# Gate and up of two feed-forwards: weights moving, three of eight feature pairs by seven block products, inner features in two halves

## Chip, cores and metric

One core of a Trainium2 chip. The metric is the device time of one execution in microseconds (us); lower is better. The core's engines are TensorE (PE in the profile, its weight loads PEld), VectorE (DVE), ScalarE (ACT), GpSimd (POOL) and SyncE (SP), whose queue issues the loads of the weights.

## What is computed

A trunk of two layers on 256 positions of 2048 features, all in float32. Layer 0 mixes by a convolution and a gating unit, layer 1 by a Fourier transform. Each is followed by the same feed-forward with 5632 inner features, and these two feed-forwards are what the change touches:

```python
def rms_norm(x, g):
    y = x * lax.rsqrt(jnp.mean(x * x, axis=-1, keepdims=True) + 1e-6)
    return y * g

def swiglu(h, w_gate, w_up, w_down):
    return (jax.nn.silu(h @ w_gate) * (h @ w_up)) @ w_down

for layer in range(2):
    x = x + mixing(rms_norm(x, mix_norm_g[layer]))          # two kinds of mixing
    h = rms_norm(x, ffn_norm_g[layer])
    x = x + swiglu(h, w_gate[layer], w_up[layer], w_down[layer])
return rms_norm(x, final_norm_g)
```

## The kernel before

Activations lie with features on the partitions: 16 feature tiles of 128 features by 256 positions (KD = 16; the inner features make KF = 44 such tiles). TensorE multiplies in a format (F32R) that holds fewer bits than float32. So each operand is split in two parts, a high part (a copy by ScalarE into that format) and a low part (VectorE: the value less its high part), and a product is high x high + high x low + low x high.

Weights come from memory in chunks of eight 128x128 tiles, 512 KB, in the order of their use. `Weights.load` (L97 to L108) takes a `raw` buffer (four of them), issues the load on SP (L104), lets ScalarE write the high part (L105) and VectorE the low part (L106). `Weights.chunk` (L133) keeps the loads three chunks ahead of the one in use, then runs `step`, which carries out small tasks that were put off (drains, norms) within a budget.

`product` (L252 to L260) makes one output tile of 128 features by 256 positions. The weight tile is stationary and the activations move. For each input tile there are two matmuls: the high weights with both parts of x side by side (512 columns, L258), and the low weights with the high part of x (256 columns, L259). The result lies in two halves of a PSUM bank, which are added when it is drained. `products` (L262) does the same with three matmuls of 256 columns. In the gating unit of layer 0, L482 to L484 work the other way round: x is stationary (128 features by 128 positions) and 512 columns of weights move, three matmuls for the three part products.

`ffn` (L327) runs over the 44 inner tiles. For each it makes a gate product and an up product over the 16 input tiles. Then `joined` (L284) adds the halves (a ScalarE copy at L287, VectorE at L289) and multiplies by the row of norm factors (L290); a sigmoid, two multiplications (L339, L340) and a split (`whole_split`, L276 and L278) make the hidden tile. All 44 stay in SBUF. After that come 16 output tiles, each a `product` over the 44 hidden tiles, added to the residual (`residual`, L316). The norm factors come late: the squares are summed on TensorE (L305), POOL takes the root (L299), and `along_free` (L308, matmuls at L312) spreads the factors along the free axis.

The code names the engine of each instruction; the order within an engine's queue is set by a planner at build time, out of the dependencies and the order in the code.

Of the kernel before, what the change touches and what calls it, by code (L numbers as in the profile page):

```python
# [17 lines left out]
ALU = mybir.AluOpType  # L21
# [14 lines left out]
NG = D // GD  # L36
NV = CD // 512
CH = 8
AHEAD = 3
RAWS, PARTS = 4, 3  # L40
NMISC = 3
PAIRS = 11
OPEN = 5
# [5 lines left out]
DELAY = 3  # L49
GAP = 2  # L50
NORM_GAP = 3
NCHUNK = (4 * KD * KC + 2 * KC * KD + KD * KD + 2 * 3 * KD * KF) // CH
RMS_EPS = 1e-6
LN_EPS = 1e-5

# [11 lines left out]
def trunk(ctx, tc, xT, vec, sgu_gb, sgu_bs, sgu_wT, w, dft_c, dft_s, out):  # L67
# [11 lines left out]

    def op(dt=F32R, shape=(P, 2 * S), name="op"):  # L80

        return acts.tile(list(shape), dt, name=name, tag="op", bufs=KF + KD)

    def tm(tag, bufs=2):
        return tmp.tile([P, S], F32, name=tag, tag=tag, bufs=bufs)

    def bank(name="m"):
        return misc.tile([P, 2 * S], F32, name=name, tag="m")

    class Weights:
        def __init__(self):
            self.loaded, self.used, self.ready = 0, 0, []
            self.tick, self.tasks, self.later, self.credit = 0, [], [], 0.0

        def load(self, pieces=1):  # L97
            raw = raws.tile([P, CH * P], F32, name="raw")
            hi = wts.tile([P, CH * P], F32R, name="whi")
            lo = wts.tile([P, CH * P], F32R, name="wlo")  # L100
            n = CH * P // pieces
            for i in range(pieces):
                c = slice(i * n, (i + 1) * n)
                nc.sync.dma_start(raw[:, c], w[self.loaded][:, c])  # L104
                nc.scalar.copy(hi[:, c], raw[:, c])  # L105
                nc.vector.tensor_sub(lo[:, c], raw[:, c], hi[:, c].bitcast(F32))  # L106
            self.loaded += 1
            self.ready.append((hi, lo))  # L108

        def start(self, task, ticks=1):  # L110

# [19 lines left out]
            self.tick += 1  # L131

        def chunk(self):  # L133
            while self.loaded < min(self.used + AHEAD + 1, NCHUNK):
                self.load()
            self.step()
            self.used += 1
            return self.ready.pop(0)

        def drain(self):  # L140
            while self.tasks or self.later:
# [174 lines left out]
    def residual(m, acc, bias=None):  # L316

        x = res[:, m, :]
        t = tm("l")
        if bias is None:  # L320
            nc.vector.tensor_add(t, acc[:, S:], x)
        else:
            nc.vector.scalar_tensor_tensor(t, acc[:, S:], bias, x, op0=ALU.add, op1=ALU.add)
        nc.vector.tensor_add(x, acc[:, :S], t)
        return x

    def ffn(norm, after, last=False):  # L327
        hs = []
        for j in range(KF):
            pg = product(norm.xs)  # L330
            pu = product(norm.xs)
            if j == 0:
                for _ in norm.factors():
                    pass
            g = joined(pg, "a", norm.R)
            u = joined(pu, "b", norm.R)
            s = tm("s", 1)
            nc.scalar.activation(s, g, AF.Sigmoid)
            nc.vector.tensor_mul(g, g, s)  # L339
            nc.vector.tensor_mul(g, g, u)  # L340
            h = op()
            whole_split(h, g)
            hs.append(h)
        for m in range(KD):
            if last and m == KD - 1:
                acc, = products(hs, 1)
                nc.vector.tensor_add(res[:, m, :], res[:, m, :], acc)
                after(m, res[:, m, :])
            else:
                after(m, residual(m, product(hs)))  # L350


    def norm_0():
# [259 lines left out]


    dr = raws.tile([P, 2, S], F32, name="raw")
    dcp = const.tile([P, 2, 2, S], F32R, name="dcp")
    dsr = raws.tile([P, 2, NB, S], F32, name="raw")
    dsp = const.tile([P, 2, NB, 2, S], F32R, name="dsp")
    nc.sync.dma_start(dr, dft_c)
    nc.sync.dma_start(dsr, dft_s)  # L620
    nc.scalar.copy(dcp[:, 0], dr)
    nc.vector.tensor_sub(dcp[:, 1], dr, dcp[:, 0].bitcast(F32))
    dcn = op(F32, (P, NB, S))
    nc.vector.tensor_copy(dcn, dsr[:, 0])
    for f in range(2):
        nc.scalar.copy(dsp[:, f, :, 0, :], dsr[:, f])
        nc.vector.tensor_sub(dsp[:, f, :, 1, :], dsr[:, f], dsp[:, f, :, 0, :].bitcast(F32))

    fx = [op() for _ in range(2 * NG)]
    nyq = acts.tile([P, NB, NG], F32, name="nyq")  # L630
# [1 line left out]
    def channels(g):  # L632
        pf = ps.tile([P, 2 * S], F32, name="acc")
        for b in range(NB):
            o = pf[:, b * S:(b + 1) * S]
            for k in range(2):
                xk = n2.xs[2 * g + k]
                xh, xl = xk[:, b * P:(b + 1) * P], xk[:, S + b * P:S + (b + 1) * P]
                nc.tensor.matmul(o, xh, dcp[:, 0, k], start=k == 0, stop=False)
                nc.tensor.matmul(o, xh, dcp[:, 1, k], start=False, stop=False)  # L640
                nc.tensor.matmul(o, xl, dcp[:, 0, k], start=False, stop=k == 1)
        return pf

    def scaled(g, pf):
# [9 lines left out]
    def positions(g, ab):  # L654
        pq = bank()
        for f in range(2):
            o = pq[:, f * S:(f + 1) * S]
            for b in range(NB):
                ah, al = ab[0][:, b, f * P:(f + 1) * P], ab[1][:, b, f * P:(f + 1) * P]
                nc.tensor.matmul(o, ah, dsp[:, f, b, 0, :], start=b == 0, stop=False)  # L660
                nc.tensor.matmul(o, ah, dsp[:, f, b, 1, :], start=False, stop=False)
                nc.tensor.matmul(o, al, dsp[:, f, b, 0, :], start=False, stop=b == NB - 1)  # L662
        return pq

    def folded(g, pq):
# [68 lines left out]
def _chunks(tiles):  # L734
    return tiles.reshape(-1, CH, P, P).transpose(0, 2, 1, 3).reshape(-1, P, CH * P)


def _cols(v):
    return np.asarray(v).reshape(-1, P).T

# [10 lines left out]
def _layout(x, mix_norm_g, ffn_norm_g, final_norm_g, ab_w_in, conv_dw_w, conv_dw_b, conv_ln_g,  # L751
            conv_ln_b, sgu_ln_g, sgu_ln_b, sgu_w, sgu_b, ab_w_out, fnet_w_out, fnet_b_out,
            ffn_w_gate, ffn_w_up, ffn_w_down):
    w = ab_w_in[0]
    pairs = np.stack([w[:, :CD].reshape(D, KC, P), w[:, CD:2 * CD].reshape(D, KC, P)], axis=2)
    pairs = pairs.reshape(D, 2 * CD)
    v = w[:, 3 * CD:].reshape(KD // 2, 2, P, NV, 512).transpose(3, 0, 2, 1, 4).reshape(-1, P, CH * P)
    fw = fnet_w_out[0].reshape(NG, GD, D)
    rows = np.concatenate([[P], np.arange(GD - 1, P, -1)])
    fw = np.concatenate([fw[:, :P].reshape(-1, D), fw[:, rows].reshape(-1, D)], axis=0)  # L760
    pairs = _chunks(_side_by_side(pairs, 2))
    wo = ab_w_out[0].reshape(2 * KC, P, KD, P).transpose(2, 0, 1, 3)
    parts = [wo[OPEN:, KC:], wo[:OPEN, KC:], wo[:OPEN, :KC - LAST], wo[:OPEN, KC - LAST:KC], wo[OPEN:, :KC]]
    wo = np.concatenate([t.reshape(-1, P, P) for t in parts])
    ws = [pairs[:24], v, pairs[24:],
          _chunks(_tiles(KD, w[:, 2 * CD:3 * CD])), _chunks(wo)]
    for layer in range(2):
        if layer:
            ws.append(_chunks(_tiles(KD, fw)))
        ws += [_chunks(_tiles(KD, ffn_w_gate[layer], ffn_w_up[layer])), _chunks(_tiles(KF, ffn_w_down[layer]))]  # L770
# [28 lines left out]
```

## Time and profile before

| | us |
|---|---|
| median of 3 runs | 1910.42 (1909.59 to 1911.05) |
| profiled execution | 1914.02 |
| its span, first to last instruction | 1912.0 |
| TensorE busy | 1888.6 (99%) |
| VectorE busy | 1279.0 (67%) |
| ScalarE busy | 985.0 (52%) |

The span is what the profiler saw of one execution; 2.0 us of that execution's time lie around it. Busy times are unions of the instructions' own spans. Matmuls overlap one another, so TensorE's pace is read from the times at which matmuls start, not from how long one lasts.

### The profile page before, as it was taken

To read this page: it belongs to the slowest core of one execution; us is meant where nothing else is said; L and a number is where in the kernel's file an instruction comes from. 1 tells how busy PE (TensorE), PEld (TensorE's weight loads), DVE (VectorE), ACT (ScalarE), POOL (GpSimd) and SP (SyncE) were. 2 spreads that over 40 slices of the span, in tenths; PEclk is the share of its full clock that TensorE was granted. 3 is DMA by queue.
4 is the path that set the end of the run, shared out by engine and by line. 5 is a ranking of instruction groups with operands and counts; after the bars stand their busy time and mean duration, and the time that the engine had idled before them with its cause. 6 is when DMAs were issued, how large, how long until landed. Compare 5 with 4: busy or idle time off the path is not lost.

```text
span 1912.0 us, 28782 instructions
## 1 busy us (share of the span) xinstructions
PE 1888.6 (99%) x11264; PEld 1672.8 (87%) x11264; DVE 1279.0 (67%) x1887; ACT 985.0 (52%) x1504; POOL 17.4 (1%) x46
## 2 busy tenths in 40 slices
PE   8999999999999999999999999999999999999997
PEld 8989988888888888888888888888888888888887
DVE  7999867666666666655555776666666666655554
ACT  8988745444444444444444654444444444444442
POOL 0000000000000000000000000000000000000000
PEclk9999999999999999999999999999999999999999
DMA  7444455555555555555556255555555555555553
GB/s 243 169 165 166 163 185 171 188 189 193 192 188 189 190 193 188 188 192 192 189 188 202 81 187 176 191 192 190 188 190 193 191 188 188 194 190 188 189 191 127
DMA packets 98319, 351.53 MB, mean 184 GB/s; under 512 B 11268, under 2 KB 12420, under 8 KB 98184
## 3 DMA queue, kind: packets, MB, share of 16 engines
q1 hardware_dynamic: 97464, 347.73, 52.8%
q8 instruction: 88, 1.44, 0.3%
q10 hardware_dynamic: 720, 1.97, 0.3%
q14 instruction: 47, 0.39, 0.1%
HBM read 347.54 MB, written 2.10 MB: 183 GB/s over the span
## 4 chain that ended last, share of the span: by engine, by line
PE 97%; DVE 1%; ACT 1%; DMA 0%; POOL 0%; issue 0%; SPq 0%; POOLq 0%; DVEq 0%; ACTq 0%
PE acc L258 56%; PE acc L259 29%; PE acc L268 3%; PE acc L269 2%; PE acc L270 2%; PE acc L482 1%; PE acc L483 1%; PE acc L484 1%; PE m L305 0%; DMA res<-in_xT 0%; PE m L312 0%; DVE wlo L106 0%; ACT whi L105 0%; PE m L660 0%; DVE res L716 0%; PE m L662 0%
## 5 line engine op out<-in xcount | busy, mean ns | idle before, releaser
L258 PE MATMUL acc<-op,whi 128*128 128x512 f32 x4692 | 1632.6, 393 | 1.4 <-ACT whi L105 1.0
L259 PE MATMUL acc<-op,wlo 128*128 128x256 f32 x4692 | 1308.3, 279 | 0.2 <-DVE wlo L106 0.2
L106 DVE TENSOR_TENSOR wlo<-raw,whi 128x1024 fp32r<-128x1024 f32 (+1 forms) x659 | 803.8, 1220 | 555.5 <-ACT whi L105 552.4
L105 ACT CAST whi<-raw 128x1024 fp32r<-128x1024 f32 (+1 forms) x659 | 688.9, 1046 | 872.6 <-issue 503.7
L258 PEld LDWEIGHTS acc<-op,whi 128*128 128x128 f32 x4692 | 879.4, 187 | 202.7 <-ACT whi L105 1.3
L259 PEld LDWEIGHTS acc<-op,wlo 128*128 128x128 f32 x4692 | 884.7, 189 | 1.2 <-DVE wlo L106 0.8
L268 PE MATMUL acc<-op,whi 128*128 128x256 f32 x428 | 125.0, 292 | 7.4 <-ACT whi L105 7.4
L269 PE MATMUL acc<-op,whi 128*128 128x256 f32 x428 | 123.2, 288 | 0.0
L270 PE MATMUL acc<-op,wlo 128*128 128x256 f32 x428 | 122.3, 287 | 0.0
L268 PEld LDWEIGHTS acc<-op,whi 128*128 128x128 f32 x428 | 84.0, 196 | 7.8 <-ACT whi L105 7.6
L269 PEld LDWEIGHTS acc<-op,whi 128*128 128x128 f32 x428 | 84.1, 196 | 0.3 <-DVE op L167 0.2
L270 PEld LDWEIGHTS acc<-op,wlo 128*128 128x128 f32 x428 | 83.5, 196 | 0.4 <-DVE wlo L106 0.3
L373 ACT ACTIVATE op<-op,vt 128x256 f32<-128x256 f32 x168 | 72.3, 498 | 0.0
L287 ACT COPY l<-acc 128x256 f32<-128x256 f32 x176 | 64.8, 368 | 0.0
L390 DVE TENSOR_TENSOR op<-op 128x512 f32<-128x512 f32 x80 | 53.8, 684 | 1.6 <-ACT op L373 1.2
L276 ACT CAST op<-a 128x256 fp32r<-128x256 f32 x112 | 44.1, 400 | 10.4 <-DVE a L541 9.4
L278 DVE TENSOR_TENSOR op<-a,op 128x256 fp32r<-128x256 f32 x112 | 46.2, 418 | 2.0 <-ACT op L276 1.8
L290 DVE TENSOR_TENSOR a<-a,nR 128x256 f32<-128x256 f32 x88 | 37.4, 426 | 6.4 <-ACT nR L210 3.5
L290 DVE TENSOR_TENSOR b<-b,nR 128x256 f32<-128x256 f32 x88 | 37.5, 426 | 3.0
L340 DVE TENSOR_TENSOR a<-a,b 128x256 f32<-128x256 f32 x88 | 37.4, 425 | 3.0
L339 DVE TENSOR_TENSOR a<-a,s 128x256 f32<-128x256 f32 x88 | 36.9, 419 | 0.0
L289 DVE TENSOR_TENSOR a<-acc,l 128x256 f32<-128x256 f32 x88 | 36.7, 418 | 0.0
(120 smaller groups left out, 720.3 us busy)
## 6 DMA issues: line engine op xcount, KB each, us to landing
raw<-in_w SPq DMA_DIRECT2D x655, 512.0 KB, 3.3
res<-in_xT SPq DMA_DIRECT2D x7, 256.0 KB, 6.8
out<-res ACTq DMA_DIRECT2D x3, 512.0 KB, 2.8
raw<-in_w SPq DMA_DIRECT2D x4, 128.0 KB, 2.6
op<-in_sgu_wT SPq DMA_DIRECT2D x2, 256.0 KB, 3.6
raw<-in_dft_s SPq DMA_DIRECT2D x1, 512.0 KB
res<-in_xT SPq DMA_DIRECT2D x2, 128.0 KB, 2.3
raw<-in_dft_c SPq DMA_DIRECT2D x1, 256.0 KB
```

The lines of the kernel that those rows point to most:

```text
L105: nc.scalar.copy(hi[:, c], raw[:, c])
L106: nc.vector.tensor_sub(lo[:, c], raw[:, c], hi[:, c].bitcast(F32))
L258: nc.tensor.matmul(acc, wh, x, start=first and k == 0, stop=False)
L259: nc.tensor.matmul(acc[:, :S], wl, x[:, :S], start=False, stop=last and k == len(xs) - 1)
L268: nc.tensor.matmul(acc, wh, x[:, :S], start=k == 0, stop=False)
L269: nc.tensor.matmul(acc, wh, x[:, S:], start=False, stop=False)
L270: nc.tensor.matmul(acc, wl, x[:, :S], start=False, stop=k == len(xs) - 1)
L278: nc.vector.tensor_sub(dst[:, n:2 * n], x, dst[:, :n].bitcast(F32))
L287: nc.scalar.copy(t, acc[:, S:])
L290: nc.vector.tensor_mul(y, y, scale)
L373: nc.scalar.activation(t[:, f * S:(f + 1) * S], src, AF.Copy, scale=wc)
L390: nc.vector.tensor_add(sums, sums, t)
```

## The change

Gate and up are worked out in 11 groups of 512 inner features for each feed-forward, in two halves of 6 and 5 groups (`HALVES`). The input tiles go in eight pairs, in the order `SEQ = "ccscscsc"`.

In a "c" pair (plain) x is stationary: for each of its two tiles, each of two blocks of 128 positions and each of gate and up, three matmuls with 512 weight columns moving. That is 24 matmuls.

An "s" pair (Strassen) takes the two feature tiles by the two blocks of positions as one 2x2 block matrix and the weights (gate | up) of the two tiles as another. It makes seven block products instead of eight, 21 matmuls. The sums of positions that this needs are built once for each feed-forward (`position_forms`); the sums of weights are built for each chunk pair while loading: the kinds "1122" (the diagonal blocks, split), "21" (one block, split), "sum" and "sum2" (VectorE adds blocks into another `raw` buffer, then the sum is split). The results go to four banks `cs` and four shared banks; after the third s pair the shared banks are combined (`sums`).

At a group's end `activate` adds `cs` and `sums`, applies the norm factor of each position and the sigmoid, and forms the product. The hidden values now have positions on the partitions, so `turned` transposes them on TensorE (8 of 128x128 a group) and splits them. That happens before the third pair of the next group. After each half the down products run over its 24 or 20 hidden tiles and are added to the residual; the first three outputs begin without the half's last group (`PARTIAL`). There are 5 `raw` buffers, 12 buffers of weight parts, and the loads run 5 units ahead, a unit being one block product of six matmuls. The row of norm factors (`along_free`) is no longer made for the feed-forward. The DFT constants move to another pool. The weights are laid out anew on the host.

```diff
-AHEAD = 3
-RAWS, PARTS = 4, 3
+AHEAD = 5
+RAWS, PARTS = 5, 12
+NOP = 53
+HALVES = (6, 5)
+SEQ = "ccscscsc"
+PARTIAL = 3
+UNITS = {"w": 2, "1122": 1, "21": 0.5, "sum": 1, "sum2": 1}
...
+        def parts_of(self, x, pieces=1):
+            hi, lo = part(), part()
+            n = CH * P // pieces
+            for i in range(pieces):
+                c = slice(i * n, (i + 1) * n)
+                nc.scalar.copy(hi[:, c], x[:, c])
+                nc.vector.tensor_sub(lo[:, c], x[:, c], hi[:, c].bitcast(F32))
+            return hi, lo
...
+            if kind == "w":
+                r = self.parts_of(self.fetch(pieces), pieces)
+            elif kind == "1122":
+                self.pair = self.fetch(), self.fetch()
+                r = self.parts_of(self.pair[0])
+            elif kind == "21":
+                x, t = self.pair[1], part()
+                nc.scalar.copy(t[:, h[0]], x[:, h[1]])
+                nc.vector.tensor_sub(t[:, h[1]], x[:, h[1]], t[:, h[0]].bitcast(F32))
+                r = t,
+            elif kind == "sum":
+                t = self.sums = raws.tile([P, CH * P], F32, name="raw")
+                two = lambda x: x.rearrange("p (o c) -> p o c", o=2)
+                b12 = self.pair[1][:, h[0]].rearrange("p (o c) -> p o c", o=1).broadcast_to([P, 2, 512])
+                nc.vector.tensor_add(two(t), two(self.pair[0]), b12)
+                r = self.parts_of(t)
+            else:
+                t = raws.tile([P, CH * P], F32, name="raw")
+                nc.vector.tensor_add(t[:, h[0]], self.sums[:, h[0]], self.pair[0][:, h[1]])
+                nc.vector.tensor_add(t[:, h[1]], t[:, h[0]], self.pair[1][:, h[1]])
+                r = self.parts_of(t)
...
+    def three(acc, x, wt, first, last):
+        for i, (f, e) in enumerate(((0, 0), (0, 1), (1, 0))):
+            nc.tensor.matmul(acc, x[f], wt[e], start=first and i == 0, stop=last and i == 2)
...
+    def hidden_group(norm, flip, before):
...
+        cs = from_ps(1) + from_misc(3) if flip else from_ps(4)
...
+            if i == 2:
+                before()
+            if c == "c":
+                for x in (xa, xb):
+                    parts = weights.chunk()
+                    for b in range(NB):
+                        for n in range(2):
+                            three(cs[2 * b + n], block(x, b), [t[:, n * 512:(n + 1) * 512] for t in parts],
+                                  i == 0 and x is xa, i == len(ORDER) - 1 and x is xb)
+            else:
+                if shared is None:
+                    shared = from_ps(4) if flip else from_ps(1) + from_misc(3)
+                p1, q5, r7, v = shared
...
+                three(p1, block(xa, 0), w11, first, last)
+                three(cs[1], d[3], w22, False, False)
+                t, = weights.chunk()
+                three(cs[0], block(xb, 0), [t[:, :512], t[:, 512:]], False, False)
...
+                three(q5, d[0], t1, first, last)
+                three(r7, d[1], t3, first, last)
...
+                three(cs[2], block(xb, 1), t4, False, False)
+                three(v, d[2], t2, first, last)
+                if last:
+                    a, y, z, zq = [op(F32) for _ in range(4)]
+                    nc.scalar.copy(a, p1)
+                    nc.vector.tensor_sub(y, v, a)
+                    nc.vector.tensor_add(z, y, r7)
+                    nc.vector.tensor_add(zq, z, q5)
+                    nc.vector.tensor_add(y, y, q5)
+                    sums = a, y, z, zq
...
+    def activate(norm, cs, sums, out):
+        for b in range(NB):
+            g, u = sums[2 * b:2 * b + 2]
+            if b == 0:
+                nc.vector.tensor_add(g, cs[0], g)
+            else:
+                nc.vector.tensor_sub(g, cs[2], g)
+            nc.vector.tensor_add(u, cs[2 * b + 1], u)
+        yield 1, 2.8
+        for b in range(NB):
+            g, u = sums[2 * b:2 * b + 2]
+            r = norm.r[:, b:b + 1]
+            sg = op(F32)
+            nc.scalar.activation(sg, g, AF.Sigmoid, scale=r)
+            nc.vector.scalar_tensor_tensor(g, g, r, sg, op0=ALU.mult, op1=ALU.mult)
+            nc.vector.scalar_tensor_tensor(g, u, r, g, op0=ALU.mult, op1=ALU.mult)
+            out.append(g)
...
     def ffn(norm, after, last=False):
-        for j in range(KF):
-            pg = product(norm.xs)
-            pu = product(norm.xs)
...
+        for half, n in enumerate(HALVES):
...
+            for g in range(n):
+                cs, sums = hidden_group(norm, g % 2, before)
+                weights.start(activate(norm, cs, sums, h))
+            k = 4 * (n - 1)
+            accs = []
+            for m in range(PARTIAL):
+                if m == PARTIAL - 1:
+                    turned(h, hs, True)
+                accs.append(product(hs[:k], last=False))
+            for m in range(KD):
...
+                    x = residual(m, product(hs[k:], accs[m], first=False) if m < PARTIAL else product(hs))
```

## Rows read from the trace of the kernel before

**Rows 1.** The page: busy us (share) and instructions; chain that ended last, by engine.
```profile
PE 1888.6 (99%) x11264; PEld 1672.8 (87%) x11264; DVE 1279.0 (67%) x1887; ACT 985.0 (52%) x1504; POOL 17.4 (1%) x46
...
PE 97%; DVE 1%; ACT 1%; DMA 0%; POOL 0%; issue 0%; SPq 0%; POOLq 0%; DVEq 0%; ACTq 0%
```

**Rows 2.** Stretches: length, busy us of PE, PEld, DVE, ACT, POOL; clock, DMA share, GB/s.
```profile
85.00:135.00 50.00, 50.00 (x241) 41.12 (x240) 48.02 (x80) 42.22 (x79) 3.05 (x3) 1.00 0.49 167
...
309.00:801.00 492.00, 490.65 (x2825) 432.35 (x2824) 332.14 (x489) 237.35 (x358) 1.65 (x1) 1.00 0.54 188
803.00:1045.00 242.00, 242.00 (x1399) 213.38 (x1398) 131.69 (x152) 103.88 (x120) 0.00 (x0) 1.00 0.56 189
...
1165.00:1655.00 490.00, 488.65 (x2823) 426.97 (x2822) 329.54 (x482) 235.61 (x353) 1.64 (x1) 1.00 0.55 189
```

**Rows 3.** Line L287 in each feed-forward: duration min/median/max ns, first and last start us.
```profile
L287 ACT COPY l<-acc x88: 365/368/368, 316.0 to 801.9; 128x256 f32<-128x256 f32 x88
...
L287 ACT COPY l<-acc x88: 362/368/369, 1170.1 to 1655.8; 128x256 f32<-128x256 f32 x88
```

**Rows 4.** Timeline (start us, us), PE in gate and up, three pairs apart.
```profile
699.90 0.39 PE L258 MATMUL acc<-op,whi 128*128 128x512 f32 x1
...
700.94 0.39 PE L258 MATMUL acc<-op,whi 128*128 128x512 f32 x1
```

**Rows 5.** Timeline, PE in the gate columns of layer 0, three matmuls apart.
```profile
99.39 0.39 PE L484 MATMUL acc<-whi,op 128*128 128x512 f32 x1
...
100.07 0.39 PE L484 MATMUL acc<-whi,op 128*128 128x512 f32 x1
```

**Rows 6.** Timeline, PE's 128-column matmuls, merged where alike and adjacent.
```profile
184.97 0.89 PE L531 MATMUL m<-op 128*128 128x128 f32 x6 [0.46 <-DVE op L411]
...
322.22 0.71 PE L312 MATMUL m<-ident,is_r 128*128 128x128 f32 x4 [1.35 <-POOL is_r L299]
```

**Rows 7.** Timeline, DVE in layer 0 where it runs without a break.
```profile
99.69 0.68 DVE L390 TENSOR_TENSOR op<-op 128x512 f32<-128x512 f32 x1
100.29 0.42 DVE L411 TENSOR_TENSOR op<-m,l 128x256 f32<-128x256 f32 x1
100.62 0.47 DVE L386 SCALAR_TENSOR_TENSOR op<-op,vt 128x256 f32<-128x256 f32 x1
101.02 1.28 DVE L390 TENSOR_TENSOR op<-op 128x512 f32<-128x512 f32 x2
102.22 1.22 DVE L106 TENSOR_TENSOR wlo<-raw,whi 128x1024 fp32r<-128x1024 f32 x1
103.36 0.87 DVE L386 SCALAR_TENSOR_TENSOR op<-op,vt 128x256 f32<-128x256 f32 x2
104.15 0.68 DVE L390 TENSOR_TENSOR op<-op 128x512 f32<-128x512 f32 x1
```

**Rows 8.** Timeline, DVE in gate and up, one inner tile.
```profile
708.83 0.42 DVE L289 TENSOR_TENSOR a<-acc,l 128x256 f32<-128x256 f32 x1
709.29 0.42 DVE L290 TENSOR_TENSOR a<-a,nR 128x256 f32<-128x256 f32 x1
...
711.61 0.42 DVE L339 TENSOR_TENSOR a<-a,s 128x256 f32<-128x256 f32 x1
...
714.38 0.42 DVE L289 TENSOR_TENSOR b<-acc,l 128x256 f32<-128x256 f32 x1
```

**Rows 9.** Groups of 309 to 801 us: busy us, mean ns, idle before, releaser.
```profile
L106 DVE TENSOR_TENSOR wlo<-raw,whi 128x1024 fp32r<-128x1024 f32 x176 | 215.7, 1226 | 152.2 <-ACT whi L105 152.1
...
L105 ACT CAST whi<-raw 128x1024 fp32r<-128x1024 f32 x177 | 186.0, 1051 | 251.9 <-issue 244.9 <-PE acc L258 7.0
```

**Rows 10.** The page, DMA issues: count, KB each, median us from issue to landing.
```profile
raw<-in_w SPq DMA_DIRECT2D x655, 512.0 KB, 3.3
```

**Rows 11.** Timeline, VectorE's result and ScalarE's copy of it.
```profile
704.20 0.43 DVE L340 TENSOR_TENSOR a<-a,b 128x256 f32<-128x256 f32 x1
...
704.79 0.40 ACT L276 CAST op<-a 128x256 fp32r<-128x256 f32 x1
```

More of the change, by code (lines that the diff above doesn't have):

```diff
@@ L88, in bank, with part @@
         return misc.tile([P, 2 * S], F32, name=name, tag="m")
+    def part():
+        return wts.tile([P, CH * P], F32R, name="part")
     class Weights:
         def __init__(self):
-            self.loaded, self.used, self.ready = 0, 0, []
+            self.loaded, self.fetched, self.ahead, self.ready = 0, 0, 0, []
             self.tick, self.tasks, self.later, self.credit = 0, [], [], 0.0
[L97 to L100, printed above, removed]
+        def parts_of(self, x, pieces=1):
+            hi, lo = part(), part()
             n = CH * P // pieces
@@ L133, in chunk @@
         def chunk(self):
-            while self.loaded < min(self.used + AHEAD + 1, NCHUNK):
+            while self.loaded < len(KINDS) and (not self.ready or
+                                                self.ahead - UNITS[self.ready[0][0]] < AHEAD):
                 self.load()
             self.step()
-            self.used += 1
-            return self.ready.pop(0)
+            kind, r = self.ready.pop(0)
+            self.ahead -= UNITS[kind]
+            return r
         def drain(self):
@@ L325, in residual, with position_forms @@
         return x
-    def ffn(norm, after, last=False):
-        hs = []
-        for j in range(KF):
-            pg = product(norm.xs)
-            pu = product(norm.xs)
[L332 to L350, printed above, removed]
+    def position_forms(key, xa, xb):
+        x, d = op(F32, (P, 4, P)), op(F32, (P, 4, P))
+        for i, t in enumerate((xa, xb)):
+            nc.vector.tensor_add(x[:, 2 * i:2 * i + 2, :].rearrange("p b c -> p (b c)"),
+                                 t[:, :S].bitcast(F32), t[:, S:].bitcast(F32))
+        yield 1, 0.84
+        for i, j in ((0, 3), (1, 0)):
+            nc.vector.tensor_sub(d[:, i, :], x[:, 1, :], x[:, j, :])
+        nc.vector.tensor_sub(d[:, 2, :], x[:, 3, :], d[:, 1, :])
+        nc.vector.tensor_sub(d[:, 3, :], x[:, 2, :], d[:, 2, :])
+        parts = op(shape=(P, 4, P)), op(shape=(P, 4, P))
+        nc.scalar.copy(parts[0], d)
+        forms[key] = parts
+        yield 1, 1.1
+        nc.vector.tensor_sub(parts[1], d, parts[0].bitcast(F32))
+        yield 1, 0.7
@@ new lines, in turned @@
+    def turned(h, hs, from_misc):
+        for i in range(2):
+            m = bank() if from_misc else ps.tile([P, 2 * S], F32, name="acc")
+            for j in range(2):
+                for b in range(NB):
+                    nc.tensor.transpose(m[:, (2 * j + b) * P:(2 * j + b + 1) * P],
+                                        h[b][:, (2 * i + j) * P:(2 * i + j + 1) * P], ident)
+            for j in range(2):
+                hs.append(op())
+                whole_split(hs[-1], m[:, j * S:(j + 1) * S])
@@ new lines, in ffn, with all_forms, before @@
+    def ffn(norm, after, last=False):
+        forms.clear()
+        def all_forms():
+            for c, (ka, kb) in ORDER:
+                if c == "s":
+                    yield from position_forms(ka, norm.xs[ka], norm.xs[kb])
+        weights.start(all_forms())
+        known = []
+        for half, n in enumerate(HALVES):
+            hs, h, final = [], [], half == len(HALVES) - 1
+            def before():
+                if not known:
+                    known.append(True)
+                    for _ in norm.factors(along=False):
+                        pass
+                if h:
+                    turned(h, hs, not g % 2)
+                    h.clear()
+            for g in range(n):
[8 more added lines that the diff above has]
+            for m in range(KD):
+                if final and last and m == KD - 1:
+                    acc, = products(hs, 1)
+                    nc.vector.tensor_add(res[:, m, :], res[:, m, :], acc)
+                else:
+                    x = residual(m, product(hs[k:], accs[m], first=False) if m < PARTIAL else product(hs))
+                if final:
+                    after(m, res[:, m, :])
@@ L735, in _chunks, with _feed_forward @@
     return tiles.reshape(-1, CH, P, P).transpose(0, 2, 1, 3).reshape(-1, P, CH * P)
+def _feed_forward(gate, up, down):
+    gate, up = [t.reshape(KD, P, -1, 512) for t in (gate, up)]
+    down = down.reshape(KF, P, KD, P)
+    chunks, g0 = [], 0
+    for n in HALVES:
+        for g in range(g0, g0 + n):
+            for c, (a, b) in ORDER:
+                if c == "s":
+                    two = (gate[a], up[b]), (up[a], gate[b])
+                else:
+                    two = (gate[a], up[a]), (gate[b], up[b])
+                chunks += [np.concatenate([t[:, g] for t in x], axis=1) for x in two]
+        h = down[4 * g0:4 * (g0 + n)].transpose(2, 0, 1, 3)
+        k = 4 * (n - 1)
+        t = [h[:PARTIAL, :k], h[:PARTIAL, k:], h[PARTIAL:]]
+        chunks += list(_chunks(np.concatenate([x.reshape(-1, P, P) for x in t])))
+        g0 += n
+    return np.stack(chunks)
 def _cols(v):
```

76 lines of the change are left out of this document (57 added, 19 removed).

## The prediction

> **What bounds the kernel now.** I read the page's busy times and chain first: TensorE is busy 99% of the span and 97% of the chain that ended last lies on it [rows 1]. So the time is TensorE's own, and the change is worth what it takes off TensorE, as long as no other engine then paces it. Next the table by stretches [rows 2]: in both gate-and-up stretches (309 to 801 and 1165 to 1655 us) PE is busy throughout at a granted clock of 1.00 and VectorE two thirds of the time (332 of 492 us); in the down stretch VectorE has 46% free.
>
> The length of gate and up comes from the copies at L287, one to each of the 88 products of a feed-forward [rows 3]: first 316.0, last 801.9, so 87 products in 485.9 us, 88 in 491.5; in the second 491.3. Together **982.7 us**. Inside, a weight tile is a 512-column and a 256-column matmul; three such pairs start within 1.04 us, 0.347 us each [rows 4]. 16 tiles x 0.347 = 5.55 us a product, 88 of them 488.6: hardly anything is waiting.
>
> **Unit of account.** The new code works in 11 groups of 512 inner features for each feed-forward, 22 in all. Before, a group's worth is 982.7 / 22 = **44.7 us**. That is the break-even.
>
> **TensorE, removed and added.** The new order (x stationary, 512 weight columns moving) is what the gate columns already do at L482 to L484: there matmuls start 0.227 us apart (99.39 to 100.07, three steps) [rows 5]. Per 1536 columns that is 0.681 us against 2 x 0.347 = 0.694, 2% for itself. A plain pair ("c") has 2 x 2 x 2 x 3 = 24 matmuls, 5.45 us; a Strassen pair ("s") has 7 x 3 = 21, 4.77 us. Group: 5 x 24 + 3 x 21 = 183 matmuls, 41.5 us. Added: 8 transposes of 128x128 in `turned`. No transpose is in the trace. Nearest rows: 128-column matmuls of split operands, six in 0.89 us, 0.12 apart, and 128-column products of plain float32, where one product is two instructions about 0.14 apart, hence 0.28 [rows 6]. A transpose is one instruction with no arithmetic to split, so I take 0.12: 1.0 us a group, bounds 0.5 (half the row, no weight-load limit) to 2.3. TensorE's group: **42.5 us**, 22 of them 935.
>
> **VectorE, which has to keep up.** Prices from a stretch where it runs without a break [rows 7], start to start: 1024 wide 1.14 us (102.22 to 103.36), 512 wide 0.60, 256 wide 0.33, scalar_tensor_tensor 256 wide 0.40 (two in 0.79), which I widen by 0.27 to 512. An operation that needs the result just ahead costs 0.46 instead of 0.33 (708.83 to 709.29) [rows 8], 0.12 more. An s pair: four of 1024 (three subtractions that split, one addition) and three of 512, 6.4 us; three pairs 19.1. Five c pairs: ten splits, 11.4. `sums` and the first half of `activate`: 8 of 512, 4.8. Second half: 4 wide scalar_tensor_tensor, 2.7. `turned`: 4 of 256, 1.3. Seven chained pairs, 0.8. Sum **40.1 us** against TensorE's 42.5: VectorE goes from two thirds to 94%, and the margin is 2.4 us a group.
>
> The margin is not even. From the c at the end of one group through the two at the start of the next, VectorE has 14.8 us of work (three c pairs, sums, activation) beside 16.3 of TensorE; in s c s c s it has 25.3 (with `turned`) beside 26.2. The lookahead of 5 units, each a product of six matmuls or 1.36 us, is 6.8 us and covers one s pair (1.6 us over). Two things eat into it. (a) Five `raw` buffers: an s pair holds four, two loads and two sums, and two of these come free only after the last addition, 4.2 us after VectorE began the pair. A load lands 3.3 us after its issue [rows 10], the copy takes 1.05 [rows 9], the split 1.14: 9.7 us from one s pair to the next, against 4.77 + 5.45 = 10.2. It fits by half a microsecond, so a load one microsecond late costs half of one. (b) All eight PSUM banks are used by a group; the next starts on banks that `sums` must have read. That chain is a copy and four operations, about 3.6 us, under 5.45 us of the last c pair. I take 0.5 us a group of TensorE waiting for (a) and (b), 11 us in all; bounds 0 (the planner hides it) and 2 us a group (44).
>
> That VectorE can stay near full beside a busy TensorE is in the trace: from 85 to 135 us it is busy 48.0 of 50 us and PE 50.0 of 50 [rows 2]. ScalarE's group: 19 copies of 1024 at 1.05 [rows 9], three of 512, and some 4 us of the rest, 26 of 42.5 us. The DMA queue moves the same bytes: 16 loads, 8.4 MB, in 42.5 us is 197 GB/s; 188 took 0.54 of the engines [rows 2].
>
> **Openings and ends.** Each feed-forward starts with `position_forms`: per pair three of 512 and four of 128, about 2.7 us, 8 us in all on VectorE, in the slot where the first group has no activation before it (7.5 us). Cost between 0 and 8; I take 2 us each, 4 in all. Gone is the wait of TensorE for the row of factors, 1.35 us at 322.2 [rows 6], already inside the 982.7. Each half ends with two partial products ahead of the transposes of its last group: 2 x 20 x 0.347 = 13.9 us in the first, 2 x 16 x 0.347 = 11.1 in the second. Activation 5.1, copies and 4 splits of coming weights 4.6 make about 10: hidden, narrowly; 0.5 us at each of four ends (0 to 2), 2 us. The second round of residual additions adds some 29 us to VectorE in the down stretches, where it has 46% free [rows 2]: nothing. The DFT constants only change pool: nothing.
>
> **Sum.** 935 + 11 + 4 + 2 = 952 us instead of 982.7: **-31 us**. The profiled execution took 1914.0 us (span 1912.0); that gives 1883. The median of the runs is 3.6 us lower, 1910.4, so I forecast 1880 us.
>
> A rule that speaks against it. Rows 7 show a 1024-wide operation that lasts 1.22 us followed by the next after 1.14. The Trainium skill, page "VectorE: DVE Perf Modes", section "The DRAIN you can't avoid", has the next operation wait until the pipe is empty, with instructions that aren't held as the exception; by the plain rule every operation costs its whole length, which is the first rival below. The exception is what rows 7 show.
>
> **Rivals.** First: VectorE pays whole durations (chained operations stand next to each other). With 1.226, 0.68, 0.42 and 0.74 us [rows 7, 9] its group is 43.2 + 0.2, above TensorE's 42.5; it then paces, and every idle half microsecond counts: 22 x 43.9 + 6 = 972, -11 us, **about 1899**. For it: the additions, `sums` and `activate` are short chains. Against: rows 7.
>
> Second, slower: VectorE stands still behind ScalarE's copy of a sum. In "sum" and "sum2" VectorE writes a tile, ScalarE copies it, VectorE subtracts. From VectorE's end to ScalarE's start is 0.16 us (704.63 to 704.79) [rows 11], the copy is 1.05, the way back 0.03: 1.24 us, six times a group. For it: these subtractions wait for that copy now, 152 us in one gate-and-up [rows 9], where it costs nothing. Against: queues are not in the order of the code. L339 of a product pair stands ahead of the L289 and L290 of its "up" half [rows 8], which the code has the other way round; so the instructions are set by readiness, and the second sum's additions can stand in the gap. All six exposed: 47.5 us a group, 22 x 47.5 + 6 = 1051, +68 us, **1978**; five, 1952. It decides from 4.3 us of idle a group (44.7 - 0.3 for openings and ends - 40.1), which is between three and four of the six.
>
> Third: the loads. If two landings in flight slow each other by 2 us, the step from s to s is 11.7, 1.5 us late three times a group; less the 1.5 us that the three c pairs leave over, 42.5 + 4.5 - 1.5 = 45.5 us a group, 22 x 45.5 + 6 = 1007, +24 us, **1935**; it goes with the second as the slower side.
>
> **How the numbers follow.** The forecast (1858 to 1893) gets 0.50: its TensorE terms are counted instructions at rows' prices. Whole durations (1893 to 1906) 0.20. No measurable change, from losses of about 1.5 to 2 us a group, 0.07. Slower by stalls of VectorE 0.23, most of it between 1915 and 1980. Faster by over 0.2% (about what a measurement of this kernel can tell from no change), that is below 1906.6: 0.70; within 0.2% 0.07; slower 0.23. Low end: no losses and cheap transposes, 22 x 42.0 + 2 = 926, -57 us, 1854; I stop at 1857. High end: 1925 takes in the mild part of the slower cases and leaves some 0.13 above.
>
> **What would show it.** Right: starts 0.227 us apart at the new product lines, about 42.5 to 43.5 us from group to group, VectorE above 90% in gate and up, PE's waits there below 20 us in a feed-forward. First rival: VectorE without idle time and PE waiting a little before each s pair. Second: VectorE's new subtractions waiting for ScalarE, above 4 us a group, and PE waiting for them. Third: ScalarE's copies waiting for the DMA of `raw`. Transposes 0.25 us apart would cost 23 us more. The forecast is wrong if a group takes more than 44.4 us.

## The result and the profile after

The changed kernel takes **1876.3 us** (median of 4 runs, 1874.5 to 1877.2) against 1910.0 us of the kernel before, run beside it (median of 4, 1909.4 to 1911.1): ratio 0.982, 95% interval 0.981 to 0.984. The forecast was 1880 us, in a range of 1857 to 1925. Beside the experiments single runs of the kernel before spread from 1908 to 1940 us, while the changed kernel, run again there, stayed within 1875.7 to 1879.2; so the experiments are compared with the changed kernel and by their own profiles, and "no gain" means against 1910 us, the low end of that spread.

The page of the changed kernel, busy time of each engine and the chain that ended last:

```profile
PE 1849.9 (99%) x9802; PEld 1584.6 (85%) x9802; DVE 1532.4 (82%) x2061; ACT 1052.6 (56%) x1444; POOL 19.8 (1%) x46
...
PE 86%; DVE 6%; DMA 4%; issue 2%; ACT 2%; SPq 0%; POOL 0%; POOLq 0%; DVEq 0%; ACTq 0%
```

Against [rows 1], PE has 1462 matmuls fewer and is still busy 99% of the span; VectorE went from 67% to 82%. A tenth of the chain now lies on VectorE and the DMA. The page's row of the weight loads, from issue to landing:

```profile
raw<-in_w SPq DMA_DIRECT2D x655, 512.0 KB, 4.3
```

A load now lands 4.3 us after its issue in the median; it was 3.3 [rows 10].

The table by stretches, changed kernel: the four stretches of gate and up, two halves in each feed-forward (length, then busy us of PE, PEld, DVE, ACT, POOL, then clock, DMA share, GB/s):

```profile
308.36:567.83 259.47, 258.38 (x1148) 209.35 (x1147) 238.45 (x294) 145.67 (x173) 1.55 (x1) 1.00 0.55 193
702.10:916.93 214.83, 212.77 (x950) 174.39 (x948) 187.77 (x218) 118.73 (x138) 0.00 (x0) 1.00 0.55 193
1148.16:1403.97 255.81, 255.69 (x1149) 210.46 (x1147) 234.72 (x288) 144.97 (x172) 1.00 (x1) 1.00 0.56 193
1538.22:1750.29 212.07, 212.05 (x949) 174.63 (x948) 188.10 (x218) 118.30 (x138) 0.00 (x0) 1.00 0.56 196
```

Together they last 942.2 us, **42.83 us a group**. Before, counted from the first gate matmul to the first down matmul (308.0 to 800.8, 1163.4 to 1654.7), the two stretches lasted 984.1 us. So gate and up gave 41.9 us. The span fell by 37.0 (1912.0 to 1875.0); the other 4.9 went elsewhere, 3.5 of them into the 32 transposes of the last groups, which stand in the down stretches. VectorE is busy 238.45 / 6 = 39.7 us a group in the first half, its opening and its end included, against two thirds of a 44.7 us group before [rows 2].

Timeline of PE in the changed kernel, transposes (L495) and products (L416):

```profile
363.06 0.38 PE L495 MATMUL acc<-ident,op 128*128 128x128 f32 x2
...
365.62 0.82 PE L495 MATMUL acc<-ident,op 128*128 128x128 f32 x6
...
431.16 0.39 PE L416 MATMUL acc<-part,op 128*128 128x512 f32 x1
431.39 0.39 PE L416 MATMUL m<-part,op 128*128 128x512 f32 x1
```

A transpose lasts 0.27 us, so six in 0.82 start 0.11 apart; the products start 0.23 apart, as the gate columns did [rows 5].

VectorE around two Strassen pairs of one group of the changed kernel (L161: addition of "sum"; L166, L167: the two of "sum2"; L131: split; L154: split of "21"):

```profile
415.74 1.22 DVE L161 TENSOR_TENSOR raw<-raw 128x1024 f32<-128x1024 f32 x1
...
425.29 1.22 DVE L161 TENSOR_TENSOR raw<-raw 128x1024 f32<-128x1024 f32 x1
426.43 0.69 DVE L154 TENSOR_TENSOR part<-raw,part 128x512 fp32r<-128x512 f32 x1
427.03 0.69 DVE L166 TENSOR_TENSOR raw<-raw 128x512 f32<-128x512 f32 x1
427.71 1.22 DVE L131 TENSOR_TENSOR part<-raw,part 128x1024 fp32r<-128x1024 f32 x1
428.86 0.68 DVE L167 TENSOR_TENSOR raw<-raw 128x512 f32<-128x512 f32 x1
430.71 1.22 DVE L131 TENSOR_TENSOR part<-raw,part 128x1024 fp32r<-128x1024 f32 x1 [1.17 <-ACT part L130]
```

Two things are to be seen. From this group's second addition to its third is 9.55 us, where 9.7 was worked out by hand; but that is one of the shorter ones. Over the 22 groups this step is 10.2 us in the median (9.3 to 15.0), and the one from a group's first addition to its second 12.9. And in the later of the two pairs, while ScalarE copies the first sum, VectorE does L154 and L166; while it copies the second, nothing else stands ready and VectorE stands for 1.17 us.

### The profile page after: what moved, and what is told of

It is laid out like the page before. It is cut to its first block, busy times and chain, and to the rows that moved or that the text cites. A ratio compares the mean times of both kernels' runs of the same rounds, so it can differ in the third digit from the quotient of the medians.

```text
span 1875.0 us, 26253 instructions
## 1 busy us (share of the span) xinstructions
PE 1849.9 (99%) x9802; PEld 1584.6 (85%) x9802; DVE 1532.4 (82%) x2061; ACT 1052.6 (56%) x1444; POOL 19.8 (1%) x46
## 4 chain that ended last, share of the span: by engine, by line
PE 86%; DVE 6%; DMA 4%; issue 2%; ACT 2%; SPq 0%; POOL 0%; POOLq 0%; DVEq 0%; ACTq 0%
PE acc L416 25%; PE acc L323 23%; PE m L416 13%; PE acc L324 12%; DMA raw<-in_w 4%; PE acc L333 2%; PE acc L334 2%; PE acc L335 2%; DVE part L131 1%; ACT part L130 1%; DVE raw L161 1%; PE acc L671 1%; PE acc L672 1%; PE acc L673 1%; DVE raw L166 1%
## 5 line engine op out<-in xcount | busy, mean ns | idle before, releaser
L130 ACT CAST part<-raw 128x1024 fp32r<-128x1024 f32 (+1 forms) x725 | 747.8, 1047 | 598.8 <-PE acc L323 288.1
L131 DVE TENSOR_TENSOR part<-raw,part 128x1024 fp32r<-128x1024 f32 (+1 forms) x725 | 872.3, 1219 | 242.1 <-ACT part L130 227.0
L323 PE MATMUL acc<-op,part 128*128 128x512 f32 x1900 | 664.0, 394 | 0.5 <-DVE op L343 0.5
L416 PE MATMUL acc<-part,op 128*128 128x512 f32 x2622 | 648.3, 391 | 0.9 <-ACT part L130 0.4
L416 PEld LDWEIGHTS acc<-part,op 128*128 128x128 f32 x2622 | 488.4, 188 | 108.3 <-ACT part L130 4.4
L324 PE MATMUL acc<-op,part 128*128 128x256 f32 x1900 | 531.9, 280 | 0.0
L323 PEld LDWEIGHTS acc<-op,part 128*128 128x128 f32 x1900 | 355.7, 187 | 82.1 <-DVE op L343 0.8
L416 PE MATMUL m<-part,op 128*128 128x512 f32 x1404 | 364.6, 391 | 0.5 <-DVE op L465 0.5
L324 PEld LDWEIGHTS acc<-op,part 128*128 128x128 f32 x1900 | 359.0, 189 | 0.5
L416 PEld LDWEIGHTS m<-part,op 128*128 128x128 f32 x1404 | 262.3, 188 | 56.9 <-DVE part L131 1.1
L333 PE MATMUL acc<-op,part 128*128 128x256 f32 x404 | 117.2, 290 | 6.5 <-ACT part L130 5.1
L335 PE MATMUL acc<-op,part 128*128 128x256 f32 x404 | 115.1, 286 | 1.2 <-DVE part L131 1.2
L334 PE MATMUL acc<-op,part 128*128 128x256 f32 x404 | 115.8, 287 | 0.0
L161 DVE TENSOR_TENSOR raw<-raw 128x1024 f32<-128x1024 f32 x66 | 80.7, 1222 | 10.7 <-DMA raw<-in_w 10.7
L333 PEld LDWEIGHTS acc<-op,part 128*128 128x128 f32 x404 | 78.6, 195 | 7.3 <-ACT part L130 5.5
L335 PEld LDWEIGHTS acc<-op,part 128*128 128x128 f32 x404 | 78.1, 194 | 1.9 <-DVE part L131 1.9
L334 PEld LDWEIGHTS acc<-op,part 128*128 128x128 f32 x404 | 78.8, 195 | 0.3 <-DVE op L232 0.2
```

Source lines behind the costliest of these rows:

```text
L130: nc.scalar.copy(hi[:, c], x[:, c])
L131: nc.vector.tensor_sub(lo[:, c], x[:, c], hi[:, c].bitcast(F32))
L161: nc.vector.tensor_add(two(t), two(self.pair[0]), b12)
L333: nc.tensor.matmul(acc, wh, x[:, :S], start=k == 0, stop=False)
L334: nc.tensor.matmul(acc, wh, x[:, S:], start=False, stop=False)
L335: nc.tensor.matmul(acc, wl, x[:, :S], start=False, stop=k == len(xs) - 1)
```

## Experiments

The theory: TensorE paces gate and up, each Strassen pair takes three matmuls a group off it, and VectorE and the raw buffers just keep up. Rivals: the gain is that of the order and the halves; VectorE paces already; VectorE stands behind ScalarE's copies.

**How much is Strassen's.** All eight pairs plain:

```diff
-SEQ = "ccscscsc"
+SEQ = "cccccccc"
...
-        return cs, sums
+        return cs, [op(F32) for _ in range(4)]
...
-            if b == 0:
-                nc.vector.tensor_add(g, cs[0], g)
-            else:
-                nc.vector.tensor_sub(g, cs[2], g)
-            nc.vector.tensor_add(u, cs[2 * b + 1], u)
+            nc.vector.tensor_copy(g, cs[2 * b])
+            nc.vector.tensor_copy(u, cs[2 * b + 1])
```

> The changed kernel with all eight pairs plain: same stationary x, same halves, same lookahead, 192 matmuls a group instead of 183. Theory (the gain is TensorE's, three matmuls less for each Strassen pair): 9 x 0.227 = 2.0 us more a group, 22 groups, +45 us, less the 7 us that the changed kernel waits on its loads: 1914 us, within 1908 to 1922, no gain over the kernel before. Rival (the gain is that of the turned-round order, the halves or the deeper buffers, the block products only shift work): below 1890 us.

Measured: 1914.3 us. Its first half by the table of stretches:

```profile
308.00:574.55 266.55, 266.55 (x1202) 221.26 (x1201) 152.19 (x165) 114.24 (x130) 1.55 (x1) 1.00 0.59 192
```

PE never idles. Without the block products nothing is left of the gain. By the profiles the four stretches of gate and up are still 8.6 us shorter than before (975.5 us against 984.1), which is what the new order leaves after paying for its transposes, and the rest of the kernel is 9.5 us longer: 3.5 are the last groups' transposes and 4.6 a slower pace of the down products of the two first halves. These take 136.54 us each here and about 134.3 in the changed kernel's profile, with the same matmuls. The same difference appears within one execution, between the two feed-forwards of the changed kernel run again (stretches of the down products of the first half):

```profile
565.42:699.68 134.26, 134.26 (x777) 118.28 (x776) 83.87 (x98) 55.13 (x56) 0.00 (x0) 1.00 0.59 197
1400.60:1537.14 136.54, 136.54 (x778) 118.59 (x776) 83.81 (x98) 54.67 (x56) 0.00 (x0) 1.00 0.58 193
```

PE is busy throughout both, at the same granted clock; most weight tiles (one L323 and one L324 matmul each) start 0.353 us apart in the slower one, 0.347 in the faster. What decides between the two paces no run shows. So of the 37.9 us that this run is longer (1914.3 against 1876.3) 33.3 lie in gate and up and are the block products'; 4.6 are this pace.

**Two pairs.**

```diff
-SEQ = "ccscscsc"
+SEQ = "ccscccsc"
```

> Two Strassen pairs of eight instead of three. Theory: three matmuls more a group, 3 x 0.227 x 22 = +15 us, less some of the waits: 1889 us, within 1884 to 1892. Rival (VectorE already paces the changed kernel, so lighter VectorE work gives time back): the same 1876 us or less.

Measured: 1885.7 us. Two pairs gave 28.5 us, 14.3 each (15.0 counted), the third 9.4. Half of that 9.4 is the pace of the down products again (136.54 us in this run too). Its first half of gate and up:

```profile
308.59:567.18 258.59, 258.59 (x1166) 214.16 (x1165) 216.65 (x261) 137.14 (x162) 1.55 (x1) 1.00 0.58 200
```

That is no longer than the 259.47 us of three pairs. All four stretches last 975.5 us with no pair, 946.1 with two and 942.2 with three: 14.7 us for each of the first two pairs, 4.0 for the third. So something took 11 us of the third pair's gain.

**Four pairs.**

```diff
-SEQ = "ccscscsc"
+SEQ = "ccsscssc"
```

> Four Strassen pairs (order ccsscssc). TensorE's group falls to 41.9 us, VectorE's work rises by 6.4 - 2.3 = 4.1 us. At start-to-start prices VectorE's group is 44.2 us and it paces: 22 x (44.2 - 42.8) = +30 us, 1906 us. At whole durations 47.9 us: +111 us, 1988 us. If VectorE doesn't pace at all: 1861 us. VectorE's idle time in gate and up should go to nearly nothing where it paces.

Measured: 1969.7 us, none of the three numbers. Stretch of the first half, and VectorE's waits in it (us in total, times, longest):

```profile
306.29:592.56 286.27, 267.35 (x1130) 207.03 (x1129) 264.69 (x333) 155.33 (x185) 2.81 (x1) 0.98 0.50 174
...
DVE part L131 <- ACT part L130: 14.8, 15, 1.2
DVE op L462 <- PE m L416: 3.4, 2, 1.8
```

VectorE's work is 264.69 / 6 = 44.1 us a group, as the start-to-start prices had it (44.2). But the group takes 47.7: VectorE sits idle for 3.6 us of it, most of that behind ScalarE's copies. It paces and yet isn't full. The order changed along with the number (two s pairs now stand side by side), and no run separates the two.

**Five pairs.**

```diff
-SEQ = "ccscscsc"
+SEQ = "ccsssssc"
```

> Five Strassen pairs (ccsssssc). Once VectorE paces, one more pair costs its own price: at start-to-start prices +4.1 us a group over four pairs, +90 us (about 1996 us); at whole durations +4.5 us, +99; if VectorE stands still behind ScalarE's copies of the two sums, 2 x 1.24 us more, +144 us.

Measured: 2055.8 us, 86.2 more than four pairs. That is nearest to the price of start to start (90), but it doesn't decide, since VectorE's idle time changes too. Its work does: four groups in the middle of the first half, from one activation to another, with three, four and five pairs:

```profile
359.14:533.62 174.48, 173.39 (x766) 138.98 (x765) 160.06 (x190) 98.74 (x116) 0.00 (x0) 1.00 0.55 193
362.11:553.75 191.64, 179.35 (x753) 139.09 (x752) 175.80 (x210) 104.45 (x124) 0.00 (x0) 0.97 0.51 176
369.32:573.65 204.33, 179.30 (x741) 131.18 (x741) 192.94 (x229) 110.63 (x132) 0.00 (x0) 1.00 0.47 165
```

VectorE's 160.06, 175.80 and 192.94 us are 40.0, 44.0 and 48.2 a group: 40.1, 44.2 and 48.3 by start-to-start prices, 43.4, 47.9 and 52.4 by whole durations. An operation that doesn't need the one ahead starts before that one has ended: in the changed kernel's timeline above, L131 at 427.71 lasts 1.22 us and L167 starts 1.15 us after it. The Trainium skill, "VectorE: DVE Perf Modes", section "The DRAIN you can't avoid", has the next operation wait for an empty pipe and lets one that isn't held start earlier; this trace shows the latter.

**Raw buffers.**

```diff
-RAWS, PARTS = 5, 12
+RAWS, PARTS = 4, 12
```

> Four raw buffers instead of five, all else as changed. Theory (the raw buffers set the step from one Strassen pair to the next): with four, nothing is prefetched beside an s pair, the first load of the next pair too waits for the pair's last addition; 9.7 us from s to s becomes about 10.7 to 11.3 against TensorE's 10.2, 0.5 to 1.1 us late three times a group, +33 to +70 us: 1909 to 1946 us. Rival (the loads have slack): 1876 to 1882 us.

Measured: 1966.2 us, 90 more, beyond the upper end. Its first half, ScalarE's waits in it, and VectorE's additions of two successive pairs:

```profile
307.10:591.79 284.69, 267.26 (x1149) 206.74 (x1147) 240.15 (x295) 147.37 (x172) 1.55 (x1) 1.00 0.51 174
...
ACT part L130 <- DMA raw<-in_w: 57.7, 66, 2.9
...
421.86 1.22 DVE L161 TENSOR_TENSOR raw<-raw 128x1024 f32<-128x1024 f32 x1
...
433.06 1.22 DVE L161 TENSOR_TENSOR raw<-raw 128x1024 f32<-128x1024 f32 x1
```

VectorE's work is nearly unchanged (240.15 us against 238.45). The step shown is 11.2 us; over the 22 groups it is 11.4 in the median instead of 10.2, and from a group's first addition to its third 25.5 instead of 23.1. TensorE needs 2 x 10.2 = 20.4 for these two steps, and the lookahead (five units of six matmuls, that is of two block products, 6.8 us) has to take up the difference. ScalarE waits 57.7 us for loads; in the changed kernel, and with six buffers (the next run), it waits in the first half

```profile
ACT part L130 <- DMA raw<-in_w: 24.6, 34, 2.2
ACT part L130 <- DMA raw<-in_w: 5.9, 8, 1.9
```

So with five buffers the loads have no slack.

**Six raw buffers**, with two operand tiles fewer to make room, and the changed kernel again as a mark.

```diff
-RAWS, PARTS = 5, 12
+RAWS, PARTS = 6, 12
-NOP = 53
+NOP = 51
```

> The changed kernel once more, on the chip and between the runs of the two below, as their mark: 1876 us within 4 us by every theory.

> Six raw buffers instead of five (two operand tiles given up for the room). Theory (the step from one Strassen pair to the next, set by the raw buffers, fits by about half a microsecond with five; what is left is 0.4 us a group of TensorE's waiting): 2 to 9 us less, 1867 to 1874 us. If five already suffice: 1876 us.

Measured: 1878.3 us for the mark, **1871.6 us** with six buffers (1870.7 to 1873.2). It beats both kernels.

```profile
308.43:563.14 254.71, 254.71 (x1148) 210.56 (x1147) 237.00 (x295) 143.48 (x174) 1.55 (x1) 1.00 0.59 196
```

254.71 / 6 = 42.45 us a group with PE busy throughout: TensorE's own time, 42.5 as counted. The four stretches last 932.5 us, so the third pair now gives 13.7 instead of 4.0: of the 11 us that it fell short by, 9.7 were the raw buffers'. From a group's first addition to its third is 21.1 us. Only 4.7 to 6.8 of the 9.7 us show in the total; in the profiles the pace of the down products hides the rest, 136.54 us in both first halves here.

**Four pairs with six raw buffers.**

```diff
-RAWS, PARTS = 5, 12
+RAWS, PARTS = 6, 12
-NOP = 53
+NOP = 51
-SEQ = "ccscscsc"
+SEQ = "ccsscssc"
```

> Four Strassen pairs as before (ccsscssc, 1970 us with five raw buffers), with six. If the idle time that VectorE kept there, 3.6 us a group, is waiting on loads and on copies that sit behind them, the group falls from 46.7 us towards its 43 to 44 us of work: 1885 to 1920 us. If that idle time is the turn-round through ScalarE, it stays at 1960 to 1970 us.

Measured: 1950.2 us, 19.4 less than with five. Neither expectation: part of the idle time was the loads, most wasn't. TensorE's clock may have a part in the 19.4: in the first half it was granted 0.98 of its full 2.4 GHz on average with five buffers, 1.00 with six. What is left, in the first half and on VectorE's timeline:

```profile
307.05:587.60 280.55, 261.97 (x1130) 203.38 (x1129) 264.20 (x333) 153.91 (x186) 2.81 (x1) 1.00 0.53 178
DVE part L131 <- ACT part L130: 14.1, 14, 1.2
...
468.25 0.68 DVE L167 TENSOR_TENSOR raw<-raw 128x512 f32<-128x512 f32 x1
470.10 1.23 DVE L131 TENSOR_TENSOR part<-raw,part 128x1024 fp32r<-128x1024 f32 x1 [1.17 <-ACT part L130]
```

**The second sum in two pieces**, on top of that.

```diff
                 nc.vector.tensor_add(t[:, h[1]], t[:, h[0]], self.pair[1][:, h[1]])
-                r = self.parts_of(t)
+                r = self.parts_of(t, 2)
```

> Four Strassen pairs with six raw buffers (1950 us, 45.8 us a group), and the second sum split in two pieces of 512, so that ScalarE can copy the first half while VectorE adds the second. Theory (what VectorE still loses there is the turn-round of 1.17 us behind the second sum's last addition, two or three times a group): the wait shrinks to about 0.3 us, two more instructions cost 0.13 us a pair: 1 to 2 us less a group, 1906 to 1930 us. Rival (VectorE's own work alone sets the 45.8 us): two more instructions for each of four pairs, 1950 to 1960 us.

Measured: 1919.7 us, 30.5 less, although VectorE has more instructions. Its first half, and its waits for ScalarE there:

```profile
306.80:579.33 272.53, 260.84 (x1130) 206.48 (x1129) 265.93 (x357) 157.00 (x211) 1.54 (x1) 0.99 0.54 184
...
DVE part L131 <- ACT part L130: 2.2, 6, 0.9
```

Against the run before, with the same six buffers, the wait fell from 14.1 us to 2.2 and the stretch from 280.55 to 272.53, while the work stayed (264.20 and 265.93). So the turn-round through ScalarE behind the second sum was what idled VectorE. With four pairs VectorE's 44.3 us of work still paces, and three pairs stay the better choice.

**GpSimd for an addition.**

```diff
-                nc.vector.tensor_add(two(t), two(self.pair[0]), b12)
+                nc.gpsimd.tensor_add(two(t), two(self.pair[0]), b12)
```

> The 1024-wide addition of the kind sum on GpSimd instead of VectorE, three Strassen pairs. VectorE loses 3 x 1.14 = 3.4 us a group. Theory (TensorE paces the changed kernel, with 0.4 us a group of waits): a gain of 0 to 9 us, 1867 to 1876 us, if GpSimd's addition takes under about 3 us. Rival (VectorE paces it already): 22 x 3.4 = 75 us less, down to TensorE's own 42.4 us a group, 1866 us. If GpSimd takes 3.6 us or more for it (128 wide it takes 0.45), the sum comes late and the time rises above 1880 us.

Measured: 1978.4 us, 102 more. GpSimd's row (count, busy us, mean ns of one) and VectorE's wait for it, over the whole span:

```profile
L161 POOL TENSOR_TENSOR raw<-raw 128x1024 f32<-128x1024 f32 x66 | 192.9, 2923 | 1267.4 <-DMA raw<-in_w 874.8 <-DVE part L131 164.1 <-DVE res L389 144.4
...
DVE raw L166 <- POOL raw L161: 94.2, 39, 4.4
```

2.9 us where VectorE takes 1.22. Under about 3 us it was to be free; it wasn't. The second sum starts from the first, so VectorE waits 94.2 us for GpSimd, and the two loads stay in their buffers meanwhile. This run lengthens the chain that holds the buffers, so it doesn't tell whether VectorE's load mattered; the six buffers do, with which TensorE never waits although VectorE's work stays (237.00 us).

**The ends of the halves.** The transposes of the last group ahead of every down product:

```diff
-PARTIAL = 3
+PARTIAL = 1
...
+                    while len(h) < NB:
+                        weights.step()
                     turned(h, hs, True)
```

> No partial products at the end of a half: the transposes of the last group stand before the first down product and wait for that group's activation. Theory (two partial products, 13.9 and 11.1 us, hide about 10 us of activation and splits): TensorE idles 6 to 10 us at each of four ends, +24 to +40 us: 1900 to 1916 us. Rival (the end is short anyway): under 1885 us.

Measured: 1888.2 us, 12 more, between the two. PE around the first end (gate and up end at 566.8):

```profile
573.54 0.40 PE L323 MATMUL acc<-op,part 128*128 128x512 f32 x1
574.01 0.44 PE L495 MATMUL m<-ident,op 128*128 128x128 f32 x2
...
574.67 0.87 PE L495 MATMUL m<-ident,op 128*128 128x128 f32 x6
```

The planner put 20 down tiles (L323) ahead of the transposes although the code has them behind. The hidden values are ready about 7 us after the half's last product, not 10, so there is little to hide: PE's waits at the four ends come to under 1 us. Most of the 12 us is pace: in all four down stretches the tiles start 0.353 us apart on average, 0.347 in the changed kernel's profile, some 7 us over the 1388 tiles. Whether the changed order brings the slower pace about, no run shows.

**Three parts** instead of two halves, with the same two added lines:

```diff
-HALVES = (6, 5)
+HALVES = (4, 4, 3)
```

> Inner features in three parts (4, 4 and 3 groups) instead of two halves. The cover of an end shrinks to 2 x 12 x 0.347 = 8.3 us, 8.3 and 5.6, against about 10 wanted: 1.7 + 1.7 + 4.4 us of TensorE's waiting in each feed-forward, +15 us, 1891 us. The third round of residual additions lies beside TensorE's down products and costs nothing. Rival (an end costs nothing, the activation is done sooner): 1876 us.

Measured: 1881.3 us, 5 more. With 7 us wanted, a cover of 8.3 us suffices, and one of 5.6 would be short by 1.4. The trace has no wait of the transposes at the two short ends; TensorE waits there, before a down product, for the first addition of the last group's activation (over the whole span: us, times, longest):

```profile
PE acc L323 <- DVE op L474: 1.9, 2, 1.2
```

The larger part of the 5 is pace again: in four of the six down stretches the tiles start 0.352 us apart, in the other two 0.347, some 5 us.

## Why the prediction was right

The mechanism and its sign were right, and the sum was off by 4 us of 1876, but some terms were mis-sized. By spans it was off by 6: 37.0 us came off where 31 were forecast, since openings and ends, 6 us in the sum, cost next to nothing.

- **TensorE's terms.** 0.227 us a matmul and 183 matmuls held: with the loads out of the way a group takes 42.4 us on average (six raw buffers, four stretches, 932.5 us in 22 groups) against 42.5 counted. The transpose, absent from the trace before, was taken at 0.12 us from [rows 6] and is 0.11. The block products alone carry the gain (no Strassen: 1914 us, as expected).
- **The start of the sum.** The 982.7 us from the copies at L287 were 1.4 us short of the 984.1 that the matmuls' own starts give: the first copy [rows 3] came late after its product.
- **TensorE's waiting.** 0.5 us a group and 4 us of openings were taken; 0.44 a group came (42.83 less 42.39), 9.7 us in all, and six raw buffers remove it all. So the raw buffers, (a), were behind it, although the trace puts TensorE's waits down to ScalarE's copies (L130), the sums (L465, which is (b)) and the activation (L485): these came late because the loads did. The openings cost nothing: with six buffers TensorE never waits in the first half, in which `position_forms` runs. That the waiting came out as taken owes something to luck: the working of (a) found that the step fits, and the 0.5 us was a choice between bounds of 0 and 2.
- **VectorE's work.** 40.1 us was counted and 40.0 is seen; with four pairs 44.2 and 44.0, with five 48.3 and 48.2. Prices taken start to start from a stretch where the engine is full [rows 7] were right, whole durations weren't.
- **VectorE's margin was mis-sized.** 2.4 us a group was called the margin. But an engine whose queue holds chains through another engine isn't free when idle: with four pairs 3.6 us of a group stayed idle while VectorE paced. The second rival had the mechanism and said that the additions of the second sum would stand in the gap. That holds for the first copy and fails for the second, behind whose last addition nothing stands ready. Three pairs just fit; had one more pair been in the change, the prediction at 1906 us would have missed by 64.
- **The raw buffers** were named as the narrow place, with half a microsecond of room (9.7 against 10.2). There was none: the step takes 10.2 in the median and the one before it 12.9, with six buffers 8.4 and 12.6. One term of the 9.7 was too small: a load was to land 3.3 us after its issue [rows 10] and took 4.3. The third rival had said 2 us more for a landing; half of that came. One buffer fewer cost 90 us where 33 to 70 were expected.
- **The ends** were costed at 2 us, on a need of 10 us; the need is about 7, the cover was ample, and PE waits at none of the four.

## What to carry to other kernels

Count the work of the engine that must keep up from start-to-start times in a stretch where it is full, and then look for chains that leave it and come back: their waits can't be filled unless something else is ready, and they come off the margin. When a step holds several buffers of a ring at once, work out the time from a buffer's release to the next use of what is loaded into it; one buffer more or less was worth 7 and 90 us here. A cut in TensorE's arithmetic pays in full only while the loads and the helper engines still keep pace, and the number of cuts is best found by running one more and one fewer. Compare such runs by the stretch that the cut touches: here two paces of an untouched stretch moved totals by 2.3 us each time, as much as some of the effects looked for.

## What the runs showed of the hardware

A 128x128 float32 transpose starts 0.11 us after the one before, less than half of a plain float32 product of the same width, which takes two instructions 0.14 apart [rows 6]. GpSimd adds two 128x1024 float32 tiles in 2.9 us on average, 2.4 times VectorE's 1.22, beside a VectorE that is nearly full. And 512-column matmuls with a new stationary operand each start 0.227 us apart over thousands of them, so the loads of the stationary operand (0.19 us each in the profile) stay beside them at that width. The same down products, two matmuls a tile, start 0.347 us a tile apart in some stretches and 0.353 in others, at the same granted clock and with TensorE never idle; it changes from stretch to stretch of one execution, and its cause is open. For the 4692 such tiles of the kernel before the slower pace would make some 30 us, an estimate from these two rates.
